# Key halves and head scaling moved between engines, scores kept negated, eps as a 129th square: a hybrid decoder layer on one core

## The chip, the core and the metric

The kernel runs on one core of one Trainium2 chip, in fp32. The metric is the device time of one execution in microseconds (us). TensorE multiplies matrices into PSUM, VectorE and ScalarE work element by element on SBUF and PSUM, GpSimd on SBUF alone, and SyncE issues most DMA transfers. In the profile these are PE, DVE, ACT, POOL and SP. Each engine takes its instructions in order from a queue of its own.

## What is computed

One layer of a decoder, for a prompt of 1024 tokens behind 16 learned meta tokens, and for 8 decoding sequences of one token each with 4096 cached positions. The part that the change touches is the differential attention of the prompt: 4 heads, each with two softmax maps over keys of width 64, values of width 128, ALiBi slopes and a causal mask. The output of each head is normalised by its root mean square.

```python
def diff_attend(q, k, v, q_pos, k_pos, lam, slopes):
    s = jnp.einsum('bqhjd,bkhjd->bhjqk', q, k) * (HEAD_DIM ** -0.5)
    s = s - slopes[None, :, None, None, None] * dist
    s = jnp.where(k_pos[None, :] <= q_pos[:, None], s, NEG_INF)
    p = jax.nn.softmax(s, axis=-1)
    a = p[:, :, 0] - lam * p[:, :, 1]
    return jnp.einsum('bhqk,bkhe->bqhe', a, v)

def diff_head_out(o, lw, li):
    o = rms_norm(o, lw['subln']) * (1.0 - lambda_init_of(li))
    return o.reshape(o.shape[:2] + (ATTN_WIDTH,))
```

The projection before it, the convolution group beside it, the output projection and the SwiGLU feed-forward part behind it, and all of the decoding, are left as they are.

## The kernel before

The kernel is written out in full, without loops on the chip. A planner orders each engine's queue from the order in which the program names the work, its dependencies and its own estimate of durations; some work (convolution, cache pages) is named with a lower or higher priority. Three stages follow one another. First the input is normalised, transposed and split, and the projections for the convolution group run (to about 150 us). Then come the attention of the prompt, 4 heads of 8 blocks of 128 queries, with the rest of the convolution, the projections of the next heads and the first cache pages of the decoding beside it (about 150 to 510 us). Then the output projection, the feed-forward part and the rest of the decoding.

Full fp32 products are made of fp32r matmuls on split operands: a number is a rounded part H plus a remainder L. For the scores, the 128 rows of the contraction hold the 64 dimensions of a map twice. L1 holds H of the scaled query on one half of the partitions and L on the other. R1 holds the rounded key on both halves, R2 the key's remainder on both. Two matmuls, L1 with R1 and L1 with R2, give all four products (lines 502 and 503).

stripe_k makes the keys of a head in 3 chunks of columns. Of each chunk and map ScalarE makes the rounded key on its own half (line 296), VectorE the same on the other half (line 297), GpSimd the remainder on its own half (line 298), and VectorE the remainder on the other half (line 299). Lines 297 and 299 depend on the projected key and on line 296 only.

attn(h, i) does one block of queries. For each map TensorE makes the scores in pieces of at most 512 keys; VectorE adds the ALiBi term, scales by the slope and keeps a running maximum (line 504). Line 510 negates the two maxima, ScalarE takes the exponential with its sum (line 512), and VectorE combines the maps: a reciprocal (514), the factor for the second map (516), and the weighted sum over all keys (520). TensorE transposes the result (528), ScalarE copies it (532), and TensorE multiplies with the values (542). The blocks stay unnormalised: what is summed is the l0-fold of the output, where l0 is the first map's sum.

After every fourth block the 4 blocks are normalised: ScalarE copies them out of PSUM (550) and sums their squares (552), VectorE forms ssq/128 + eps*l0*l0 in two steps (556, 557), GpSimd takes the power -1/2 (559), and VectorE scales each block by it and by the weight row subln (561). Four blocks are one tile of 128x512, from a pool of 8 that other tiles use too. head_out transposes them (569), copies them out (571) and stores them; it is called in the next head's or half's work.

Beside this GpSimd multiplies cache pages with the decoding queries (line 677, two pages at a time), VectorE sums them (687), and the convolution's taps run on ScalarE (408), GpSimd (409) and VectorE (418). att_consts loads the weight row subln over all partitions and the page table early in the first stage (lines 366 to 369).

Of the kernel before, what the change touches and what calls it, by code (L numbers as in the profile page):

```python
# [16 lines left out]
P = 128  # L17
# [24 lines left out]
SLAB = 1056  # L42


@with_exitstack
def tile_layer(ctx: ExitStack, tc: tile.TileContext, I, O, cfg):
# [23 lines left out]
    def att(name, dt=F32):  # L70
        return at.tile([P, 512], dt, tag="at", name=name)
# [36 lines left out]
    subln = cst.tile([P, P], F32, name="subln")  # L108
    convb = cst.tile([P, 4], F32, name="convb")
# [174 lines left out]
    def stripe_k(h):  # L284
# [5 lines left out]
        for c, o in proj(HL, f"pk{h}"):  # L290
            key_evac(k, o, c, 4 + h, "s")
            c0, w = CHUNKS[c]
            d = slice(max(c0 - DB, 0), c0 + w - DB)
            for j in range(2):
                sl, ot = slice(j * HD, (j + 1) * HD), slice((1 - j) * HD, (2 - j) * HD)
                S.copy(R1s[j][sl, d], k[sl, d])
                V.tensor_copy(R1s[j][ot, d], k[sl, d])
                (G if cfg["r2_g"] else V).tensor_tensor(R2s[j][sl, d], k[sl, d], R1s[j][sl, d].bitcast(F32), op=ALU.subtract)
                V.tensor_tensor(R2s[j][ot, d], k[sl, d], R1s[j][sl, d].bitcast(F32), op=ALU.subtract)
            if c < 2:  # L300
                yield
# [64 lines left out]
    def att_consts():  # L366
        bcast_row(subln, I["subln_w"][0])
        V.tensor_scalar(subln, subln, 1.0 - LAM_INIT, None, op0=ALU.mult)
        D.dma_start(pts, I["page_table"].rearrange("(o b) n -> o (b n)", o=1))
# [111 lines left out]
    def attn(h, i):  # L481
        W = META + P * (i + 1)
        qs = slice(i * P, (i + 1) * P)
        if i == 0:
            att_st["l"] = smt(f"l{h}", 16, 2)
            att_st["ssq"] = smt(f"ssq{h}", 8, 2)
            if h == 0:
                att_st["junk"] = smt("junk", P, 1)
# [7 lines left out]
        mx = smt(f"mx{h}{i}", 2, 4)  # L496
        for j in range(2):
            p = slp.tile([P, NKEY], F32, tag="p", name=f"p{h}{i}{j}", bufs=cfg["p"])
            for a in range(0, W, w):
# [5 lines left out]
                    out=p[:, a:e], in0=o, in1=bias[:, b0 + a : b0 + e], scale=SLOPES[h],  # L505
                    scalar=NEG if a == 0 else mx[:, j : j + 1], op0=ALU.add, op1=ALU.max, accum_out=mx[:, j : j + 1],
                )
            pj.append(p)
        nm = smt(f"nm{h}{i}", 2, 4)
        V.tensor_scalar(nm, mx, -1.0, None, op0=ALU.mult)  # L510
        for j in range(2):
            S.activation(pj[j][:, :W], pj[j][:, :W], AF.Exp, bias=nm[:, j : j + 1], accum_out=lh[:, 2 * i + j : 2 * i + j + 1])
        rl = smt(f"rl{h}{i}", 1, 4)
        V.reciprocal(rl, lh[:, 2 * i + 1 : 2 * i + 2])
        cc = smt(f"cc{h}{i}", 1, 4)
        V.scalar_tensor_tensor(cc, lh[:, 2 * i : 2 * i + 1], neglam, rl, op0=ALU.mult, op1=ALU.mult)
# [30 lines left out]
        if i % 4 == 3:  # L547
            oh = att(f"oh{h}{i}")
            b0 = i - 3
            S.copy(oh, o)  # L550
            for b in range(4):
                S.activation(att_st["junk"], oh[:, b * P : (b + 1) * P], AF.Square, accum_out=ssq[:, b0 + b : b0 + b + 1])
            bs = slice(b0, i + 1)
            l0 = lh.rearrange("p (i j) -> p i j", j=2)[:, bs, 0]
            t1 = smt(f"t1{h}{i}", 4)
            V.scalar_tensor_tensor(t1, l0, EPS, l0, op0=ALU.mult, op1=ALU.mult)
            V.scalar_tensor_tensor(t1, ssq[:, bs], 1.0 / P, t1, op0=ALU.mult, op1=ALU.add)
            r = smt(f"or{h}{i}", 4)
            G.tensor_tensor(r, t1, mhalf[:, :4], op=ALU.pow)
            for b in range(4):  # L560
                V.scalar_tensor_tensor(
                    oh[:, b * P : (b + 1) * P], oh[:, b * P : (b + 1) * P], r[:, b : b + 1], subln,
                    op0=ALU.mult, op1=ALU.mult,
                )

            def head_out():
                pt = pb(f"oT{h}{i}")
                for b in range(4):
                    T.transpose(out=pt[:, b * P : (b + 1) * P], in_=oh[:, b * P : (b + 1) * P], identity=ident)
                m = att(f"mo{h}{i}")  # L570
                S.copy(m, pt)
# [860 lines left out]
```

## Time and profile before

| | |
|---|---|
| median of 3 runs | 1490.66 us (1486.98 to 1492.48) |
| the profiled execution | 1491.31 us |
| its span, from the first to the last instruction | 1489.3 us |
| busy: TensorE, VectorE, ScalarE, GpSimd | 1375.3, 964.9, 514.8, 562.6 us |
| mean granted TensorE clock | 0.960 |

The busy times are those of the span. The profile names instructions by line of the kernel and by tile (out<-in), and says for idle time which engine's instruction ended it. A line's duration includes what an instruction waits after its start. The granted clock is the share of full speed that TensorE had. The chain of waits is followed back from the last instruction: at each step to what released it, or to the instruction before it on its engine.

### The profile page before, as it was taken

Reading aid. Unit: us, or ns where it says so; the run is one execution under the profiler, and the core shown is the slowest. Engines: PE = TensorE matmul, PEld = TensorE weight load, DVE = VectorE, ACT = ScalarE, POOL = GpSimd, SP = SyncE. Lnnn points to the kernel's source line nnn. Section 1 sums busy time; section 2 is a strip of 40 time slices with the busy share of each in tenths; the row PEclk is TensorE's granted clock in tenths of the full one; section 3 lists DMA queues with packets and bytes.
Section 4 is the critical chain, followed back from the end, with each engine's and each line's share of the span. In section 5 each row is a group of like instructions: output and inputs, shape, how many; then the busy total and the mean of one; then the engine's idle time right before and its main releaser. Section 6 shows DMA issues by size and latency. Waiting matters only on the chain.

```text
span 1489.3 us, 21639 instructions
## 1 busy us (share of the span) xinstructions
PE 1375.3 (92%) x6960; PEld 1071.5 (72%) x6960; DVE 964.9 (65%) x1531; ACT 514.8 (35%) x1021; POOL 562.6 (38%) x351
## 2 busy tenths in 40 slices
PE   6999678888875899999999999999999999999997
PEld 6999678877864778777776776767676666566666
DVE  5689998894888456855665747575654176353158
ACT  6566565547555324511312012211112112112122
POOL 3698663542425211363554445455540000000014
PEclk9999899998886899999999999999999999999999
DMA  8211012422424554768886777677676735763454
GB/s 263 72 44 45 15 44 93 121 85 92 156 81 148 181 173 136 268 214 255 278 267 208 250 244 246 235 258 267 216 253 225 260 122 192 261 192 124 162 182 173
DMA packets 199534, 264.35 MB, mean 178 GB/s; under 512 B 16279, under 2 KB 99672, under 8 KB 199413
## 3 DMA queue, kind: packets, MB, share of 16 engines
q1 hardware_dynamic: 188768, 254.40, 52.2%
q10 hardware_dynamic: 10653, 8.57, 1.8%
q8 instruction: 55, 0.90, 0.2%
q14 instruction: 58, 0.48, 0.1%
HBM read 245.92 MB, written 17.48 MB: 177 GB/s over the span
## 4 chain that ended last, share of the span: by engine, by line
PE 68%; DVE 16%; issue 5%; DMA 4%; ACT 3%; SPq 2%; POOL 1%; DVEq 0%; POOLq 0%; ACTq 0%
PE pg L147 6%; PE pg L148 6%; PE pg L149 6%; PE pu L147 5%; PE pu L148 5%; PE pu L149 5%; PE dn L147 5%; PE dn L148 5%; PE dn L149 5%; PE pv L729 4%; DVE p L504 2%; PE mo L149 2%; PE mo L147 2%; PE mo L148 2%; DVE acc L418 2%
## 5 line engine op out<-in xcount | busy, mean ns | idle before, releaser
L677 POOL TENSOR_TENSOR k<-k,qB 128x1024 f32<-128x1024 f32 x128 | 320.5, 2518 | 269.1 <-DMA k<-in_cache_k 227.6
L687 DVE TENSOR_REDUCE s<-k 128x16 f32<-128x1024 f32 x128 | 154.8, 1212 | 99.8 <-POOL k L677 95.0
L953 ACT CAST wH<-wr 128x1024 fp32r<-128x1024 f32 x66 | 69.0, 1048 | 251.9 <-DVE wL L955 148.9
L147 PE MATMUL dn<-wH,aH 128*128 128x512 f32 x352 | 141.6, 406 | 4.2 <-DVE y L996 2.6
L147 PE MATMUL pu<-hH,wH 128*128 128x512 f32 x352 | 141.0, 401 | 1.3 <-DVE y L996 1.3
L149 PE MATMUL pu<-hH,wL 128*128 128x512 f32 x352 | 139.7, 398 | 1.5 <-DVE sm2n_t L121 1.5
L148 PE MATMUL dn<-wL,aH 128*128 128x512 f32 x352 | 140.9, 400 | 0.0
L148 PE MATMUL pu<-hL,wH 128*128 128x512 f32 x352 | 140.1, 399 | 0.0
L147 PE MATMUL pg<-hH,wH 128*128 128x512 f32 x352 | 140.1, 398 | 0.0
L149 PE MATMUL dn<-wH,aL 128*128 128x512 f32 x352 | 140.0, 398 | 0.0
L148 PE MATMUL pg<-hL,wH 128*128 128x512 f32 x352 | 139.6, 396 | 0.0
L149 PE MATMUL pg<-hH,wL 128*128 128x512 f32 x352 | 139.5, 396 | 0.0
L955 DVE TENSOR_TENSOR wL<-wr,wH 128x1024 fp32r<-128x1024 f32 x66 | 104.4, 1582 | 43.8 <-ACT wH L953 23.6
L996 DVE TENSOR_TENSOR y<-dn,y 128x512 f32<-128x512 f32 x144 | 95.0, 682 | 33.7 <-PE dn L149 33.4
L409 POOL TENSOR_TENSOR cb<-cb 128x512 f32<-128x512 f32 x80 | 103.6, 1325 | 26.5 <-ACT cb L408 14.2
L418 DVE SCALAR_TENSOR_TENSOR acc<-u,cw,acc 128x512 f32<-128x512 f32 x144 | 99.5, 748 | 0.3
L1068 POOL TENSOR_TENSOR y<-y,wfpost 128x512 f32<-128x512 f32 x10 | 17.3, 1747 | 207.1 <-ACT ft L1066 207.0
L147 PEld LDWEIGHTS dn<-wH,aH 128*128 128x128 f32 x352 | 67.6, 192 | 30.7 <-issue 6.9
L147 PEld LDWEIGHTS pu<-hH,wH 128*128 128x128 f32 x352 | 66.6, 189 | 28.8 <-issue 12.0
L148 PEld LDWEIGHTS dn<-wL,aH 128*128 128x128 f32 x352 | 67.2, 191 | 24.4 <-issue 10.3
L147 PEld LDWEIGHTS pg<-hH,wH 128*128 128x128 f32 x352 | 66.2, 188 | 24.9 <-issue 9.0
L148 PEld LDWEIGHTS pu<-hL,wH 128*128 128x128 f32 x352 | 66.5, 189 | 24.2 <-issue 10.3
(582 smaller groups left out, 2986.5 us busy)
## 6 DMA issues: line engine op xcount, KB each, us to landing
k<-in_cache_k SPq DMA_DIRECT2D x256, 256.0 KB
v<-in_cache_v SPq DMA_DIRECT2D x256, 256.0 KB
wr<-in_w_gate SPq DMA_DIRECT2D x22, 512.0 KB
wr<-in_w_up SPq DMA_DIRECT2D x22, 512.0 KB
wr<-in_w_down SPq DMA_DIRECT2D x22, 512.0 KB
sd<-in_w_down SPq DMA_DIRECT2D x22, 512.0 KB
sw_gate<-in_w_gate SPq DMA_DIRECT2D x20, 512.0 KB
sw_up<-in_w_up SPq DMA_DIRECT2D x20, 512.0 KB
```

Source lines behind the costliest of these rows:

```text
L147: T.matmul(out, lhsT=wH, rhs=xH, start=first, stop=False)
L148: T.matmul(out, lhsT=wH, rhs=xL, start=False, stop=False)
L149: mark(T.matmul(out, lhsT=wL, rhs=xH, start=False, stop=last))
L409: G.tensor_tensor(accp, accp, t, op=ALU.add)
L418: V.scalar_tensor_tensor(dst, src, cw[:, ct, k : k + 1], acc, op0=ALU.mult, op1=ALU.add)
L504: V.tensor_tensor_reduce(out=p[:, a:e], in0=o, in1=bias[:, b0 + a : b0 + e], scale=SLOPES[h], scalar=NEG if a == 0 else mx[:, j : j + 1], ...
L677: x = G.tensor_tensor(kt, kt, qB.unsqueeze(1).to_broadcast([P, 2, 512]), op=ALU.mult)
L687: x = V.tensor_reduce(s.rearrange("p a c -> p (a c)"), kt.rearrange("p a (c d) -> p (a c) d", d=HD), axis=AX.X, op=ALU.add)
L729: x = T.matmul(pv[32 * g : 32 * g + 8, :], lhsT=a[:, q + i, :], rhs=vt[:, i, :], start=q + i < 4, stop=q + i >= NPG - 4, tile_position=(0, ...
L953: S.copy(H[:, :1024], raw[:, :1024])
L955: V.tensor_tensor(L[:, :1024], raw[:, :1024], H[:, :1024].bitcast(F32), op=ALU.subtract)
L996: V.tensor_tensor(y[b][:, ws], o, y[b][:, ws], op=ALU.add)
```

## The change

The second halves of the key operands: line 297's copy goes from VectorE to ScalarE, reading the key as before. Line 299's subtraction on VectorE becomes a copy by ScalarE of what GpSimd's subtraction (line 298) gave on the other half. GpSimd keeps that subtraction.

The scores are kept with the sign turned: the slope is negative, the running maximum becomes a running minimum of the negated scores, which is the bias that the exponential needs; the exponential takes a scale of -1. Line 510 goes. The factor of line 516 is formed with two per-partition scalars instead of a scalar and a second tensor.

The normalisation: a tile of 4 x 132 columns with 2 buffers of its own holds the 4 blocks. ScalarE writes sqrt(128*eps)*l0 behind each block's 128 columns, and the square sums 129 columns, so that the power takes the sum as it is; lines 556 and 557 go. The factor sqrt(128) moves into the weight. ScalarE scales each block by the power (instead of VectorE, line 561). The weight subln, now one value a partition (a new load of 128 values and one multiplication in att_consts), is applied in the copy behind the transposition (line 571). The row form of subln stays, for the decoding.

```diff
--- before.py
+++ after.py
@@ -40,6 +40,7 @@
 C0 = CHUNKS[0][1]
 KT = [(0, META)] + [(META + P * i, P) for i in range(NB)]
 SLAB = 1056
+OHW = P + 4
 
 
 @with_exitstack
@@ -106,6 +107,7 @@
         D.dma_start(dst, row.partition_broadcast(P))
 
     subln = cst.tile([P, P], F32, name="subln")
+    sublnT = cst.tile([P, 1], F32, name="sublnT")
     convb = cst.tile([P, 4], F32, name="convb")
     clnw = cst.tile([P, 4], F32, name="clnw")
     clnb = cst.tile([P, 4], F32, name="clnb")
@@ -294,9 +296,9 @@
             for j in range(2):
                 sl, ot = slice(j * HD, (j + 1) * HD), slice((1 - j) * HD, (2 - j) * HD)
                 S.copy(R1s[j][sl, d], k[sl, d])
-                V.tensor_copy(R1s[j][ot, d], k[sl, d])
-                (G if cfg["r2_g"] else V).tensor_tensor(R2s[j][sl, d], k[sl, d], R1s[j][sl, d].bitcast(F32), op=ALU.subtract)
-                V.tensor_tensor(R2s[j][ot, d], k[sl, d], R1s[j][sl, d].bitcast(F32), op=ALU.subtract)
+                S.copy(R1s[j][ot, d], k[sl, d])
+                G.tensor_tensor(R2s[j][sl, d], k[sl, d], R1s[j][sl, d].bitcast(F32), op=ALU.subtract)
+                S.copy(R2s[j][ot, d], R2s[j][sl, d].bitcast(F32))
             if c < 2:
                 yield
         for pt, ts, name in key_tiles(k, f"kn{h}"):
@@ -366,6 +368,9 @@
     def att_consts():
         bcast_row(subln, I["subln_w"][0])
         V.tensor_scalar(subln, subln, 1.0 - LAM_INIT, None, op0=ALU.mult)
+        with nc.allow_non_contiguous_dma("128 values, once"):
+            D.dma_start(sublnT, I["subln_w"][0].rearrange("(p o) -> p o", o=1))
+        S.mul(sublnT, sublnT, (1.0 - LAM_INIT) * P ** 0.5)
         D.dma_start(pts, I["page_table"].rearrange("(o b) n -> o (b n)", o=1))
 
     def conv_consts():
@@ -485,7 +490,7 @@
             att_st["l"] = smt(f"l{h}", 16, 2)
             att_st["ssq"] = smt(f"ssq{h}", 8, 2)
             if h == 0:
-                att_st["junk"] = smt("junk", P, 1)
+                att_st["junk"] = smt("junk", P + 1, 1)
         lh, ssq = att_st["l"], att_st["ssq"]
         L1s, R1s, R2s = heads[h]["L1"], heads[h]["R1"], heads[h]["R2"]
         bias = att_st["alibi"]
@@ -493,7 +498,7 @@
         np_ = -(-W // 512)
         w = -(-W // np_ // 8) * 8
         pj = []
-        mx = smt(f"mx{h}{i}", 2, 4)
+        nm = smt(f"nm{h}{i}", 2, 4)
         for j in range(2):
             p = slp.tile([P, NKEY], F32, tag="p", name=f"p{h}{i}{j}", bufs=cfg["p"])
             for a in range(0, W, w):
@@ -502,18 +507,19 @@
                 T.matmul(o, lhsT=L1s[j][:, qs], rhs=R1s[j][:, a:e], start=True, stop=False)
                 T.matmul(o, lhsT=L1s[j][:, qs], rhs=R2s[j][:, a:e], start=False, stop=True)
                 V.tensor_tensor_reduce(
-                    out=p[:, a:e], in0=o, in1=bias[:, b0 + a : b0 + e], scale=SLOPES[h],
-                    scalar=NEG if a == 0 else mx[:, j : j + 1], op0=ALU.add, op1=ALU.max, accum_out=mx[:, j : j + 1],
+                    out=p[:, a:e], in0=o, in1=bias[:, b0 + a : b0 + e], scale=-SLOPES[h],
+                    scalar=-NEG if a == 0 else nm[:, j : j + 1], op0=ALU.add, op1=ALU.min, accum_out=nm[:, j : j + 1],
                 )
             pj.append(p)
-        nm = smt(f"nm{h}{i}", 2, 4)
-        V.tensor_scalar(nm, mx, -1.0, None, op0=ALU.mult)
         for j in range(2):
-            S.activation(pj[j][:, :W], pj[j][:, :W], AF.Exp, bias=nm[:, j : j + 1], accum_out=lh[:, 2 * i + j : 2 * i + j + 1])
+            S.activation(
+                pj[j][:, :W], pj[j][:, :W], AF.Exp, scale=-1.0, bias=nm[:, j : j + 1],
+                accum_out=lh[:, 2 * i + j : 2 * i + j + 1],
+            )
+        cc = smt(f"cc{h}{i}", 1, 4)
         rl = smt(f"rl{h}{i}", 1, 4)
         V.reciprocal(rl, lh[:, 2 * i + 1 : 2 * i + 2])
-        cc = smt(f"cc{h}{i}", 1, 4)
-        V.scalar_tensor_tensor(cc, lh[:, 2 * i : 2 * i + 1], neglam, rl, op0=ALU.mult, op1=ALU.mult)
+        V.tensor_scalar(cc, lh[:, 2 * i : 2 * i + 1], neglam, rl, op0=ALU.mult, op1=ALU.mult)
         A = pj[0]
         cut = META + 3 * P
         for a, e in (((0, cut), (cut, W)) if W > cut and cfg["asp"] else ((0, W),)):
@@ -545,30 +551,26 @@
                 )
         mark(x)
         if i % 4 == 3:
-            oh = att(f"oh{h}{i}")
+            oh = at.tile([P, 4 * OHW], F32, tag="oh", name=f"oh{h}{i}", bufs=2)
+            ov = oh.rearrange("p (b e) -> p b e", e=OHW)
             b0 = i - 3
-            S.copy(oh, o)
-            for b in range(4):
-                S.activation(att_st["junk"], oh[:, b * P : (b + 1) * P], AF.Square, accum_out=ssq[:, b0 + b : b0 + b + 1])
+            S.copy(ov[:, :, :P], o.rearrange("p (b e) -> p b e", e=P))
             bs = slice(b0, i + 1)
             l0 = lh.rearrange("p (i j) -> p i j", j=2)[:, bs, 0]
-            t1 = smt(f"t1{h}{i}", 4)
-            V.scalar_tensor_tensor(t1, l0, EPS, l0, op0=ALU.mult, op1=ALU.mult)
-            V.scalar_tensor_tensor(t1, ssq[:, bs], 1.0 / P, t1, op0=ALU.mult, op1=ALU.add)
+            S.mul(ov[:, :, P], l0, (P * EPS) ** 0.5)
+            for b in range(4):
+                S.activation(att_st["junk"], ov[:, b, : P + 1], AF.Square, accum_out=ssq[:, b0 + b : b0 + b + 1])
             r = smt(f"or{h}{i}", 4)
-            G.tensor_tensor(r, t1, mhalf[:, :4], op=ALU.pow)
+            G.tensor_tensor(r, ssq[:, bs], mhalf[:, :4], op=ALU.pow)
             for b in range(4):
-                V.scalar_tensor_tensor(
-                    oh[:, b * P : (b + 1) * P], oh[:, b * P : (b + 1) * P], r[:, b : b + 1], subln,
-                    op0=ALU.mult, op1=ALU.mult,
-                )
+                S.mul(ov[:, b, :P], ov[:, b, :P], r[:, b : b + 1])
 
             def head_out():
                 pt = pb(f"oT{h}{i}")
                 for b in range(4):
-                    T.transpose(out=pt[:, b * P : (b + 1) * P], in_=oh[:, b * P : (b + 1) * P], identity=ident)
+                    T.transpose(out=pt[:, b * P : (b + 1) * P], in_=ov[:, b, :P], identity=ident)
                 m = att(f"mo{h}{i}")
-                S.copy(m, pt)
+                S.mul(m, pt, sublnT)
                 if h < NH - 1:
                     S.dma_start(mixT[h, :, b0 * P : (i + 1) * P], m)
                 else:
```

## Rows read from the trace of the kernel before

**Rows 1.** Stretch: us, busy PE, PEld, DVE, ACT, POOL (count), clock, DMA share, GB/s.

```profile
0.00:150.00 150.00, 135.85 (x851) 132.24 (x851) 113.82 (x202) 94.54 (x157) 105.07 (x99) 0.98 0.35 105
150.00:510.00 360.00, 282.32 (x1684) 260.77 (x1685) 296.90 (x630) 201.14 (x506) 160.12 (x105) 0.87 0.31 98
510.00:1489.30 979.30, 957.12 (x4427) 678.47 (x4425) 554.20 (x700) 219.09 (x359) 297.44 (x148) 0.99 0.66 218
```

**Rows 2.** The same view, first and last part of the attention stage.

```profile
150.00:220.00 70.00, 51.09 (x283) 46.69 (x283) 69.29 (x130) 41.31 (x96) 45.08 (x34) 0.88 0.11 31
...
450.00:500.00 50.00, 30.58 (x154) 26.17 (x155) 38.15 (x72) 22.64 (x53) 26.49 (x13) 0.66 0.39 133
```

**Rows 3.** Chain of waits, shares by line, in 150:220 and in 220:510.

```profile
by line: DVE acc L418 38.1%; issue 12.2%; DVE p L504 11.1%; DVE R L297 9.0%; DVE R L299 7.6%; DVE nm L510 6.6%; DVE p L520 6.0%; DVE acc L416 2.9%; DVE L L268 2.1%; DVE acc L410 2.0%; DVE u L418 1.2%; DVE cc L516 0.9%; DVE rl L514 0.6%; DVE
...
by line: issue 11.7%; DVE p L504 8.1%; DVE p L520 6.6%; PE o L542 5.1%; ACT p L512 4.9%; DVE R L299 4.8%; DVE cc L516 4.2%; DVE R L297 3.6%; DVE oh L561 3.2%; DVE s L687 2.9%; PE AT L528 2.5%; PE S L502 1.9%; DMA k<-in_cache_k 1.8%; ACT u L
```

**Rows 4.** Who waited for whom, 150:510: us in total, times, longest.

```profile
ACT p L512 <- DVE nm L510: 43.4, 20, 9.4
...
PE S L502 <- DVE mx L504: 20.7, 13, 4.6
...
POOL k L677 <- DMA k<-in_cache_k: 21.1, 1, 21.1
...
DVE t L557 <- ACT junk L552: 12.9, 4, 5.8
...
ACT cb L408 <- POOL cb L409: 3.5, 6, 0.9
```

**Rows 5.** VectorE groups, 150:510: count | busy us, mean ns | idle before, releaser.

```profile
L520 DVE SCALAR_TENSOR_TENSOR p<-p,cc,p 128x400 f32<-128x400 f32 (+7 forms) x52 | 40.8, 816 | 0.5
...
L299 DVE TENSOR_TENSOR R<-kT,R 64x384 fp32r<-64x384 f32 (+1 forms) x24 | 22.7, 946 | 0.7
...
L516 DVE SCALAR_TENSOR_TENSOR cc<-l,neglam,rl 128x1 f32<-128x1 f32 x32 | 20.2, 631 | 0.3
...
L297 DVE CAST R<-kT 64x384 fp32r<-64x384 f32 (+1 forms) x24 | 19.5, 817 | 0.6
...
L561 DVE SCALAR_TENSOR_TENSOR oh<-oh,or,subln 128x128 f32<-128x128 f32 x32 | 16.7, 583 | 2.4 <-POOL or L559 2.3
...
L510 DVE TENSOR_SCALAR nm<-mx 128x2 f32<-128x2 f32 x32 | 16.7, 525 | 0.3
...
L557 DVE SCALAR_TENSOR_TENSOR t<-ssq,t 128x4 f32<-128x4 f32 x8 | 5.4, 674 | 12.9 <-ACT junk L552 12.9
...
L556 DVE SCALAR_TENSOR_TENSOR t<-l 128x4 f32<-128x4 f32 x8 | 4.5, 558 | 2.6 <-ACT p L512 2.6
```

**Rows 6.** Single lines: count, shortest/median/longest ns, first and last start, forms.

```profile
L297 DVE CAST R<-kT x24: 296/791/2521, 150.9 to 412.3; 64x384 fp32r<-64x384 f32 x16, 64x272 fp32r<-64x272 f32 x8
...
L510 DVE TENSOR_SCALAR nm<-mx x32: 149/170/2379, 166.9 to 476.7; 128x2 f32<-128x2 f32 x32
...
L561 DVE SCALAR_TENSOR_TENSOR oh<-oh,or,subln x32: 339/347/2431, 220.9 to 505.6; 128x128 f32<-128x128 f32 x32
...
L121 DVE TENSOR_SCALAR hr_t<-hs x8: 135/154/155, 515.9 to 603.2; 128x1 f32<-128x1 f32 x8
```

**Rows 7.** ScalarE groups as in rows 5; the last as in rows 6.

```profile
L296 ACT CAST R<-kT 64x384 fp32r<-64x384 f32 (+1 forms) x24 | 11.3, 480 | 0.5
...
L552 ACT ACTIVATE junk<-oh 128x128 f32<-128x128 f32 x32 | 9.9, 308 | 1.5 <-ACT junk L552 1.0
...
L436 ACT ACTIVATE u<-yT,ln0n,ln_r x4: 450/457/460, 240.1 to 241.1; 128x128 f32<-128x128 f32 x4
```

**Rows 8.** GpSimd groups, 150:510, as in rows 5.

```profile
L677 POOL TENSOR_TENSOR k<-k,qB 128x1024 f32<-128x1024 f32 x25 | 59.5, 2389 | 28.3 <-DMA k<-in_cache_k 21.1 <-issue 7.0
...
L298 POOL TENSOR_TENSOR R<-kT,R 64x384 fp32r<-64x384 f32 (+1 forms) x24 | 23.5, 984 | 43.5 <-ACT R L296 35.4 <-PE S L502 7.4
```

**Rows 9.** ScalarE timeline around 56 us: start, us, instruction, idle before and releaser.

```profile
55.91 1.05 ACT L136 CAST wi8H<-wi8r 128x1024 fp32r<-128x1024 f32 x1 [2.96 <-DMA wi8r<-in_w_in]
```

## Prediction

> **What bounds the kernel now.** I read the busy times by stretch first. After 510 us TensorE is busy 957 of 979 us at a granted clock of 0.99; up to 150 us it is busy 136 of 150. Between them, 150 to 510 us, where the four heads' attention runs beside the convolution and the first cache pages, it is busy 282 of 360 at 0.87, while VectorE has 297 (82%), ScalarE 201 (56%) and GpSimd 160 (44%) [rows 1]. Everything the change touches but one load runs in that stretch, so only this stage is to be judged. At its start it is plain who sets the pace: in 150 to 220 us VectorE is busy 69.3 of 70 us. [...]
>
> The chain of waits says the same. In the first 70 us it goes through VectorE nearly throughout, from 220 on mostly through VectorE, with pieces of TensorE and ScalarE between [rows 3]. And the waits show the direction: TensorE waits for the scores' reduction to free PSUM (20.7 us for its scores alone), ScalarE waits 43.4 us in 20 places for the negated maximum; ScalarE waits for GpSimd hardly at all (3.5 us in 6 places, in the convolution's taps) [rows 4]. So VectorE is the engine to relieve here, and ScalarE has about 159 us free.
>
> **What VectorE loses.** Within 150 to 510 us: L297 19.5 us, L299 22.7, L510 16.7, L561 16.7, L556 4.5 and L557 5.4 go; together 85.5 us. L516 stays as an instruction without a second tensor; a 128x1 tensor_scalar took at most 155 ns [rows 6], so its 20.2 us may become 32 x 0.155 = 5.0, a gain of 15.2 (bounds 0 and 15.2) [rows 5]. Sum 100.7 us of 297.
>
> But most of that is waiting inside the instruction. L510, two elements wide, takes 149 ns at best and 2379 at worst; L297 296 to 2521; L561 339 to 2431 [rows 6]. The long ones have the length of GpSimd's page product, 2389 ns [rows 8]. By the shortest durations the removed work is 48 key copies and subtractions x 0.296 = 14.2, 32 x 0.149 = 4.8 for L510, 16 x 0.149 = 2.4 for L556 and L557, 32 x 0.339 = 10.8 for L561, together 32 us; L516 would gain about nothing. So 32 us is work, and 100.7 - 32 = 69 us is waiting for GpSimd, a wait that can pass on to the next instruction of the same kind. L520 is that next one: it stands right behind L516, has two SBUF inputs, and has 52 instructions of mean 816 ns [rows 5]. I take it that a third of the waits move there: 212 instructions (those of rows 5) shrink to 52, but the 52 meet the same GpSimd work.
>
> [...]
>
> **What ScalarE gains.** A 64-partition cast of the same shape takes it 480 ns [rows 7]. The first copy: 24 x 0.48 = 11.5. The second, from the subtraction's result: 24 x 0.48 = 11.5. The heads' scaling, 32 pieces of 128x128 with a per-partition scale: between the square with no such operand, 308 ns, and the normalisation with two, 457 ns; I take the middle, 0.38, so 12.2 (9.9 to 14.6). The scaled row sum, 8 pieces, at most as long as the square: 2.5. The copy after the transposition gets a per-partition scale: 8 x 0 to 0.15, 0.6. Sum 38 us, into 159 free.
>
> **Costs near nothing.** The exponential takes an immediate scale of -1 and a minimum takes the place of a maximum: same instruction, same count. Eps goes into a 129th column of the square, 1 element more. GpSimd keeps its 24 subtractions (984 ns) and 8 powers; each power is now released by ScalarE's sum and no longer by L557, which waited 12.9 us for that sum [rows 4]. One new load, 128 values on SyncE's queue among the loads of the first 60 us, and one ScalarE multiplication that waits for it: the nearest row is ScalarE's wait of 2.96 us for a weight block at 56 us [rows 9]; 0 to 3 us, and TensorE, 136 of 150 us busy there with projections, has work queued, so I take 0. If that cover is gone it costs those 3 us.
>
> **The new waits.** L299 needed only ScalarE's first copy. Now ScalarE's second copy waits for GpSimd's subtraction, and the scaling waits for GpSimd's power; behind either, in ScalarE's queue, stand the exponentials and the copies of transposed weights, for which TensorE waits. There are 24 + 8 such handovers. From below: ScalarE lost 3.5 us in 6 places over the taps, where its multiplications alternate with GpSimd's sums [rows 4], and VectorE 2.3 us before L561 [rows 5]; the planner that orders each queue puts other work between. From above: each of 12 chunks (4 heads, 3 chunks) holds ScalarE for two subtractions, 12 x 1.97 = 24 us. I take 5, well inside the 43 us that ScalarE idled for L510.
>
> **The sum.** What the chain loses: in 150 to 220 us L297 9.0%, L299 7.6%, L510 6.6% and L516 0.9%, 24.1% of 70 = 16.9 us; in 220 to 510, L299 4.8%, L516 4.2%, L297 3.6% and L561 3.2%, 15.8% of 290 = 45.8 us [rows 3]. Together 62.7; of L516's 12.8 a quarter remains as work, so 59.5. Of this, work and the two thirds of waits that vanish: (32 + 46) / 100.7 x 59.5 = 46 us. What comes back: 38 + 5 us on ScalarE, which ends at about (201 + 43) / 323 = 76% busy, below VectorE's old 82%; I put a quarter of the 38 on the path, 9 us, the handovers being inside it (bounds 0 and 43). 46 - 9 = 37 us. The profiled execution took 1491.3 us, 1489.3 of it span; its place against the median of the runs, 1490.7, is 0.6 above. 1491.3 - 37 = 1454 us. After 510 TensorE is full, so what the stage saves should stay saved to the end; the page loads are paced by TensorE's work and run at 0.66 share there [rows 1].
>
> **The rivals.**
> Waits move on: all 69 us of waiting reappear at L520 and its like. Then the chain loses 32 / 100.7 x 59.5 = 19 us, less 9 to 15 on ScalarE: 1482 to 1487, say 1485. For it: nothing about GpSimd's work changes. Against it: three quarters of the instructions that can meet it go.
>
> ScalarE takes VectorE's place: the 43 us lie on its path nearly in full, 46 - 37 = 9 us left: 1482. For it: the subtraction's handover is in the loop of each key chunk, and head 0's are needed at once. Against it: 159 us free.
>
> Slower: ScalarE stops behind a page. GpSimd's queue holds 25 page products; one waited 21.1 us for its page [rows 4, 8]. If a subtraction or power of the above stands behind such a product, ScalarE stands still too, and with it exponentials and transposes. Each costs about 21.1 + 2.4 = 23.5 us. One leaves the forecast at 1478; from two on the gain of 37 is eaten: 2 x 23.5 - 37 = +10, 1501. For it: a shorter stage asks for pages earlier. Against it: once in 25 so far.
>
> More: nothing comes back, 60 us, 1431. TensorE would then run its 282 us, fewer at a better clock, in 300, which the stage after 510 shows to be possible.
>
> The change doesn't do what it says: if ScalarE's half copies or scaled pieces took twice the rows' durations, nothing would be left, 1491; a 64-partition row of the same shape makes that unlikely.
>
> **How the numbers follow.** Forecast 0.57 (about 1437 to 1473); waits move on 0.11; ScalarE in VectorE's place 0.10; more 0.11; slower 0.09; not as said 0.02. The range reaches from the end of "more" to that of "waits move on", 1428 to 1486, and leaves out the slower rival and the tails. A measurement of this kernel can tell about 0.5%, 7.5 us: faster means under 1483, slower over 1498. Faster: 0.57 + 0.11 + half of the two small-gain rivals, 0.11 = 0.79; within: 0.10 + 0.02 = 0.12; slower 0.09.
>
> **What would show it.** Right: in the attention stage VectorE's busy time falls by 70 to 90 us, ScalarE's rises by about 38, the wait of the exponentials falls far below 43 us, the stage ends 37 us earlier, at about 473, and the time after it stays 979 us. L516 stays near 0.15 us with no long cases. L520's mean shows how much waiting moved: 816 ns plus a third of 69 us over 52, some 1250; twice that would be the second rival. ScalarE's waits for GpSimd before the second copies and before the scaling show the handovers: 5 us expected, one stop over 15 us would be the slower rival at work. Wrong: the stage ends early but the part after it grows, or TensorE's idle time in the stage stays at 78 us under another name, say transposed weights' copies or a half clock through the end of the stage.

## The result and the profile after

The changed kernel took 1449.2 us (median of 4 executions, 1442.3 to 1453.7), the kernel before 1488.8 beside it: a ratio of 0.973, with an interval of 0.968 to 0.978. That is 39.6 us faster; the forecast was 1454, 37 us under the profiled execution of before. The profiled execution of the changed kernel is the fastest of its four, 1442.3 us, and that of before, 1491.3 us, lies 2.5 us above the median, so differences between the two traces come out some 9 us larger than those of the medians (49.0 against 39.6).

I take as the end of the attention stage the last transposition of normalised heads. Before, it started at 510.7 us and ended at 511.0; now it ends at 464.4. These are its rows before and after (shortest/median/longest ns, first and last start):

```profile
L569 PE MATMUL oT<-ident,oh x32: 270/418/475, 234.7 to 510.7; 128*128 128x128 f32 x32
...
L571 PE MATMUL oT<-ident,oh x32: 270/273/475, 216.7 to 464.1; 128*128 128x128 f32 x32
```

The busy times of the changed kernel in the attention stage and after it, columns as in rows 1:

```profile
150.00:464.40 314.40, 264.22 (x1700) 247.87 (x1699) 220.53 (x506) 239.71 (x599) 164.03 (x108) 0.93 0.36 114
464.40:1440.63 976.23, 954.05 (x4420) 675.41 (x4419) 544.46 (x700) 219.07 (x359) 292.79 (x147) 0.99 0.66 218
```

And the kernel before over its own stage, so that the same work is compared:

```profile
150.00:511.00 361.00, 283.32 (x1690) 261.63 (x1691) 297.30 (x631) 201.14 (x506) 160.98 (x106) 0.87 0.31 97
```

The stage lasts 314 us instead of 361, and the rest 976 instead of 978: in these two executions what the stage saved stayed saved. In the stage VectorE is busy 77 us less, ScalarE 39 us more, GpSimd 3 us more, and the granted clock is 0.93 instead of 0.87, so that TensorE does the same work in 264 us instead of 283. After the change TensorE is busy 84% of the stage, ScalarE 76%, VectorE 70%.

Groups of VectorE in the changed kernel's stage, which answer to rows 5 (line 526 was 520, line 522 was 516, line 432 belongs to the convolution's layer norm):

```profile
L526 DVE SCALAR_TENSOR_TENSOR p<-p,cc,p 128x400 f32<-128x400 f32 (+7 forms) x52 | 45.1, 898 | 0.7
...
L522 DVE TENSOR_SCALAR cc<-l,neglam,rl 128x1 f32<-128x1 f32 x32 | 8.5, 266 | 0.6
...
L702 DVE COPY s<-selfs 128x8 f32<-128x8 f32 x3 | 2.4, 870 | 0.0
...
L432 DVE SCALAR_TENSOR_TENSOR ln4n<-ln4m,ln_r 128x1 f32<-128x1 f32 x1 | 2.3, 2333 | 0.2 <-POOL ln_r L125 0.2
...
L432 DVE SCALAR_TENSOR_TENSOR ln3n<-ln3m,ln_r 128x1 f32<-128x1 f32 x1 | 2.3, 2331 | 0.2 <-POOL ln_r L125 0.2
...
L432 DVE SCALAR_TENSOR_TENSOR ln6n<-ln6m,ln_r 128x1 f32<-128x1 f32 x1 | 2.3, 2320 | 0.2 <-POOL ln_r L125 0.2
```

The weighted sum rose from 816 to 898 ns only. Line 522 has no long cases left, but costs 266 ns rather than 155. Some long cases turned up in places nobody named: three one-column instructions of the layer norm take 2.3 us now (before, one of them took 2.3 us, the same line for the decoding 2.2 and another 1.2), and copies of 8 columns 870 ns on average instead of 158.

Groups of ScalarE, answering to rows 7 (298, 299 and 301 are the key halves, 566 the scaling, 573 the copy with the weight; 150 to 470 us):

```profile
L301 ACT CAST R<-R 64x384 fp32r<-64x384 f32 (+1 forms) x24 | 11.5, 481 | 0.6
...
L299 ACT CAST R<-kT 64x384 fp32r<-64x384 f32 (+1 forms) x24 | 11.5, 481 | 0.6
...
L298 ACT CAST R<-kT 64x384 fp32r<-64x384 f32 (+1 forms) x24 | 11.5, 481 | 0.4
...
L566 ACT ACTIVATE oh<-oh,or 128x128 f32<-128x128 f32 x32 | 10.3, 393 | 6.1 <-POOL or L564 6.1
...
L573 ACT ACTIVATE mo<-oT,sublnT 128x512 f32<-128x512 f32 x8 | 5.5, 690 | 5.8 <-PE oT L571 5.8
```

And the waits that answer to rows 4:

```profile
ACT p L515 <- DVE nm L509: 19.4, 12, 5.3
...
DVE p L509 <- PE S L508: 33.2, 16, 8.5
...
PE S L507 <- DVE nm L509: 15.1, 7, 5.2
...
ACT oh L566 <- POOL or L564: 6.1, 3, 4.2
```

This is the kernel before for the second of them:

```profile
DVE p L504 <- PE S L503: 8.0, 7, 2.4
```

The exponentials wait 19 us for VectorE instead of 43. VectorE now waits 33 us for scores from TensorE instead of 8; TensorE still waits 15 us for VectorE's reduction, 21 before. ScalarE waits for GpSimd's power 6.1 us in 3 places, and before line 301, which waits for GpSimd's subtraction, 0.6 us in all.

### The profile page after: what moved, and what is told of

Its sections match the earlier page's. It is cut to its first block, busy times and chain, and to the rows that moved or that the text cites. A ratio compares the mean times of both kernels' runs of the same rounds, so it can differ in the third digit from the quotient of the medians.

```text
span 1440.6 us, 21580 instructions
## 1 busy us (share of the span) xinstructions
PE 1353.5 (94%) x6960; PEld 1054.5 (73%) x6960; DVE 876.8 (61%) x1403; ACT 552.2 (38%) x1112; POOL 560.5 (39%) x351
## 4 chain that ended last, share of the span: by engine, by line
PE 61%; DMA 2%; issue 2%; DVE 2%; SPq 2%; POOL 1%; ACT 0%; POOLq 0%; DVEq 0%; ACTq 0%
PE pg L149 5%; PE pu L149 5%; PE pg L150 5%; PE pu L150 5%; PE pu L151 5%; PE pg L151 5%; PE dn L149 5%; PE dn L150 5%; PE dn L151 5%; PE pv L731 4%; PE mo L151 2%; PE mo L149 2%; PE mo L150 2%; DMA k<-in_cache_k 1%; POOL k L679 1%
## 5 line engine op out<-in xcount | busy, mean ns | idle before, releaser
L957 DVE TENSOR_TENSOR wL<-wr,wH 128x1024 fp32r<-128x1024 f32 x66 | 97.1, 1471 | 38.0 <-ACT wH L955 21.6
L998 DVE TENSOR_TENSOR y<-dn,y 128x512 f32<-128x512 f32 x144 | 95.0, 684 | 35.4 <-PE dn L151 34.9
L981 ACT CAST aH<-sg 128x512 fp32r<-128x512 f32 x44 | 27.3, 621 | 163.2 <-DVE sg L974 163.1
L150 PEld LDWEIGHTS dn<-wL,aH 128*128 128x128 f32 x352 | 66.9, 190 | 25.1 <-issue 10.3
```

The lines of the kernel that those rows point to most:

```text
L150: T.matmul(out, lhsT=wH, rhs=xL, start=False, stop=False)
L957: V.tensor_tensor(L[:, :1024], raw[:, :1024], H[:, :1024].bitcast(F32), op=ALU.subtract)
L981: S.copy(aH, sg)
L998: V.tensor_tensor(y[b][:, ws], o, y[b][:, ws], op=ALU.add)
```

## Experiments

The theory to be tested: VectorE's queue sets the pace of the attention stage, so what leaves VectorE shortens it, until another engine takes over. Rivals: the waits for GpSimd only move to the next instruction; ScalarE takes VectorE's place; or the planner's new order moves the time by itself, whatever the edit. Times are medians; the difference is to the kernel before on the same chip, whose medians in the four sets of runs lie between 1488.8 and 1491.5 us. Stage ends and busy times are those of one execution of each kernel, the profiled one; the stage ends with the last transposition of heads.

### Each part alone

**Key halves alone** (b_keys): of the diff only

```diff
-                V.tensor_copy(R1s[j][ot, d], k[sl, d])
+                S.copy(R1s[j][ot, d], k[sl, d])
...
-                V.tensor_tensor(R2s[j][ot, d], k[sl, d], R1s[j][sl, d].bitcast(F32), op=ALU.subtract)
+                S.copy(R2s[j][ot, d], R2s[j][sl, d].bitcast(F32))
```

> The kernel before with the key halves' part alone (lines 297 and 299 by ScalarE). Theory of the prediction (VectorE's queue sets the pace of the attention stage, two thirds of the waits for GpSimd vanish): these lines held 36 us of the chain, so 36 x 0.77 = 28 us less, and 6 us back on ScalarE: 22 us faster than before. Waits move on to the weighted sum: only the work goes, about 6 us faster. Planner's order alone: anything within 10 us either way, unrelated to the part's size.

1450.6 us, 40.9 less (ratio 0.973, 0.971 to 0.975). This one part gives as much as the whole change, within the intervals. The stage ends at 472.1; its row:

```profile
150.00:472.10 322.10, 273.11 (x1700) 253.83 (x1699) 249.00 (x585) 230.19 (x563) 164.27 (x108) 0.90 0.34 111
```

VectorE is busy 48 us less in it, more than the 42 of the two lines. The gain is nearly twice the 22 us expected.

**Negated scores alone** (b_neg):

```diff
-                    scalar=NEG if a == 0 else mx[:, j : j + 1], op0=ALU.add, op1=ALU.max, ...
+                    scalar=-NEG if a == 0 else nm[:, j : j + 1], op0=ALU.add, op1=ALU.min, ...
...
-        V.tensor_scalar(nm, mx, -1.0, None, op0=ALU.mult)
```

with the negative slope and the exponential's scale of -1 as in the whole change.

> The kernel before with the negated scores alone (line 510 gone). Theory of the prediction: about 4 to 6 us faster, the exponentials' wait for VectorE falls from 43 us, and most of line 510's 16.7 us leaves VectorE. Waits move on: line 516 and the weighted sum take over what line 510 waited for GpSimd, under 2 us faster. Planner's order alone: within 10 us either way.

1473.1 us, 18.4 less (0.989, 0.987 to 0.991), three to four and a half times what was expected. The stage ends at 490.3:

```profile
150.00:490.30 340.30, 278.58 (x1690) 257.36 (x1691) 283.27 (x599) 201.15 (x506) 164.48 (x106) 0.89 0.32 104
```

VectorE lost 14 of line 510's 16.8 us; the stage became 21 us shorter. The wait of the exponentials, which was to fall, hardly changed (43.4 to 41.8 us). That speaks for VectorE's time as what counted, and not for the negation's place before the exponential:

```profile
ACT p L510 <- DVE nm L504: 41.8, 24, 5.3
```

**Line 516 alone** (b_cc):

```diff
-        V.scalar_tensor_tensor(cc, lh[:, 2 * i : 2 * i + 1], neglam, rl, op0=ALU.mult, op1=ALU.mult)
+        V.tensor_scalar(cc, lh[:, 2 * i : 2 * i + 1], neglam, rl, op0=ALU.mult, op1=ALU.mult)
```

> The kernel before with line 516 alone changed to two per-partition scalars. Theory of the prediction: its mean falls from 631 ns to about 155, some 7 us faster. Waits move on: its mean falls too, but the weighted sum's mean rises by as much in total, from 816 to about 1100 ns, and the time stays as it was. Planner's order alone: within 10 us either way.

1481.0 us, 10.5 less (0.993, 0.991 to 0.995). Its instructions (shortest/median/longest ns) and the weighted sum's group:

```profile
L516 DVE TENSOR_SCALAR cc<-l,neglam,rl x32: 257/271/274, 179.0 to 473.7; 128x1 f32<-128x1 f32 x32
...
L520 DVE SCALAR_TENSOR_TENSOR p<-p,cc,p 128x400 f32<-128x400 f32 (+7 forms) x52 | 42.4, 842 | 0.4
```

No case over 274 ns, where the old form had taken up to 2415; and the weighted sum right behind it went from 816 to 842 ns, 1.4 us in total. Here the wait did not move to the next instruction. The mean of line 516 was to fall to 155 ns and fell to 270. The stage ends at 501.2, VectorE is busy 289.3 us in it, 8.0 less than before.

**Normalisation alone** (b_heads):

```diff
-                V.scalar_tensor_tensor(
-                    oh[:, b * P : (b + 1) * P], oh[:, b * P : (b + 1) * P], r[:, b : b + 1], subln,
+                S.mul(ov[:, b, :P], ov[:, b, :P], r[:, b : b + 1])
...
-                S.copy(m, pt)
+                S.mul(m, pt, sublnT)
```

and lines 556 and 557 gone, with the 129th column and the new tile as in the whole change.

> The kernel before with the normalisation's part alone (eps in the square sum, scaling by ScalarE, the weight behind the transposition). Theory of the prediction: line 561 held 9.3 us of the chain, so 9.3 x 0.77 = 7 us less and 3 us back on ScalarE, 4 us faster, and lines 556 and 557 a little more. Waits move on: 3 us faster at most. ScalarE in VectorE's place: the wait of the scaling for GpSimd's power stops the exponentials, no gain or up to 5 us slower.

1485.3 us, 6.2 less (0.996, 0.994 to 0.997). The stage ends at 500.1, 11 us earlier, with VectorE busy 289.7 us; the rest took 984 instead of 978. Here most of what left VectorE came back: the lines taken out held 26.6 us (16.7, 5.4 and 4.5), VectorE is only 7.7 us lighter, and the weighted sum alone rose by 10.9 us, from 816 to 1023 ns:

```profile
L525 DVE SCALAR_TENSOR_TENSOR p<-p,cc,p 128x400 f32<-128x400 f32 (+7 forms) x52 | 51.7, 1023 | 0.7
```

The four add up to 76 us, the whole change gives 40. They are not independent.

### The planner's order, and a wait taken out by itself

**Another pool** (b_pool): nothing moves between engines.

```diff
-            oh = att(f"oh{h}{i}")
+            oh = at.tile([P, 512], F32, tag="oh", name=f"oh{h}{i}", bufs=2)
```

> The kernel before with nothing moved: only the tile of the four heads' blocks comes from two buffers of its own instead of the common eight. If the planner's order by itself moves the time by 5 to 10 us, as the differences between the parts might suggest, this shows it. Theory now (the gains come from VectorE's queue): within 4 us of before.

1489.0 us against 1489.8: 0.9999 (0.998 to 1.002). The queues are ordered anew, the stage ends at 508.4 instead of 511.0, VectorE is busy 299.8 us, and the time stays. That is one order among many, but it gives no support to the planner as the cause of 10 to 40 us. It also shows how much a new order alone shifts: 2.5 us of VectorE's busy time.

**Line 510 without its waits** (b_nm2):

```diff
-        V.tensor_scalar(nm, mx, -1.0, None, op0=ALU.mult)
+        for j in range(2):
+            V.tensor_scalar(nm[:, j : j + 1], mx[:, j : j + 1], -1.0, None, op0=ALU.mult)
```

> The kernel before with line 510's one instruction on two columns made two instructions on one column each: more work for VectorE (32 more instructions of about 0.15 us), but a one-column tensor_scalar took at most 155 ns before. If waiting for GpSimd in line 510 is what cost time: the long cases go, busy time of the line falls from 16.7 to about 10 us, and 4 to 12 us of the 18 that leaving the line out gained. If the line's work, its place in VectorE's queue, cost the time: 2 to 5 us slower than before. If waits move on: the long cases go to line 516 and the weighted sum, no change or slightly slower.

1491.2 us against 1489.8, 1.0014 (0.9995 to 1.003): no gain. Its 64 instructions, and its stage, which ends at 505.6:

```profile
L511 DVE TENSOR_SCALAR nm<-mx x64: 127/146/156, 159.5 to 473.8; 128x1 f32<-128x1 f32 x64
```

```profile
150.00:505.60 355.60, 283.36 (x1695) 262.66 (x1694) 295.44 (x664) 207.76 (x514) 166.16 (x108) 0.88 0.30 99
```

The long cases went entirely: none over 156 ns, where the two-column instruction had reached 2379 [rows 6]. By the prediction's count 12 us of waiting (16.8 less 32 x 0.149) were taken out and 4.6 us of work put in (64 x 0.146 against 32 x 0.149), which should leave VectorE 7.5 us lighter. It is 1.9 us lighter: some 5.6 us, nearly half of the waits, came back elsewhere, in the weighted sum among others (905 ns), though a new order alone moved VectorE's busy time by 2.5 us in b_pool. So the length of a line in the profile, waits included, is not what one gains by taking out its waits alone. The stage ended 5.4 us earlier all the same, and the rest took 982 instead of 978 us; of a difference of this size in the stage the time shows nothing.

### What sets the pace afterwards

**Whole change without the key halves** (a_keys_v), **without the normalisation** (a_heads_v), **without the negated scores** (a_nm): the diffs above, turned round.

> The changed kernel with lines 297 and 299 back on VectorE, the other three parts kept. The parts alone gave 41 (keys), 18 (negated scores), 10 (line 516) and 6 us (normalisation) against the kernel before, together 76, while all four gave 40 to 42. Theory now: VectorE sets the pace only until enough is off it, then TensorE and ScalarE do; the three other parts still find VectorE full, so they add up nearly, 27 to 35 us under before: about 1460. If instead each part's time is the planner's luck, the result is anywhere between 1445 and 1490.

1458.4 us, 33.1 less than before (0.977, 0.974 to 0.980). The stage ends at 470.2, with VectorE busy 34 us less than before:

```profile
150.00:470.20 320.20, 267.24 (x1690) 250.32 (x1691) 263.31 (x552) 214.92 (x549) 167.57 (x106) 0.91 0.35 114
470.20:1455.35 985.15, 956.49 (x4420) 678.15 (x4418) 541.23 (x700) 219.25 (x359) 295.06 (x147) 0.99 0.65 216
```

> The changed kernel with the normalisation as before (scaling by VectorE, lines 556 and 557 back), the other three parts kept. Theory now: VectorE has room, ScalarE gets 13 us back: the same as the changed kernel within 4 us, 1445 to 1453. If ScalarE sets the pace now: 6 to 10 us faster than the changed kernel. If VectorE still sets it: 6 us slower, as the part alone gained.

1455.0 us, 36.5 less (0.976, 0.973 to 0.978); the stage ends at 474.7, VectorE busy 252.4 us:

```profile
150.00:474.70 324.70, 267.57 (x1693) 248.46 (x1692) 252.44 (x552) 227.44 (x558) 164.33 (x107) 0.93 0.34 109
```

"The same within 4 us" was missed: it is 5.8 us slower than the changed kernel and its stage 10.3 us longer, nearly the 10.9 that the part alone had taken off the stage, as was expected if VectorE still set the pace.

> The changed kernel with line 510's negation and the maximum back, the other three parts kept. Theory now: VectorE has room, so most of the 18 us that this part gained alone is not lost again, but the negation lies in the path from scores to exponential: 2 to 8 us slower than the changed kernel. If VectorE still sets the pace: 15 to 18 us slower.

1456.1 us, 35.4 less (0.976, 0.973 to 0.979). In its stage and rest:

```profile
150.00:465.70 315.70, 266.04 (x1690) 248.22 (x1691) 225.45 (x535) 233.33 (x593) 162.56 (x106) 0.91 0.36 115
465.70:1453.93 988.24, 958.45 (x4420) 678.63 (x4419) 543.81 (x700) 218.97 (x359) 295.72 (x147) 0.99 0.65 215
```

The three lie within 10 us of the changed kernel, and their intervals overlap its own. Still, the changed kernel with more work for ScalarE (a_act2, the next experiment), measured beside them, took 1447.1 to 1451.8 us, and every execution of the three lies above that (1452.2 to 1460.4). So each of these parts is worth some 6 to 10 us in the whole, though the three together add nothing to the key halves alone that can be measured. The negation, worth 21 us of stage alone, costs 1 us of stage here (465.7 against 464.4). What a_nm and a_keys_v lose besides lies after the stage: 988 and 985 us instead of 976. TensorE waits there longer for the value pages; these are the rows of a_nm, a_keys_v and the changed kernel, and then of a_act2 and a_heads_v, between 511 and 1440 us:

```profile
PE pv L730 <- DMA v<-in_cache_v: 11.7, 4, 3.7
```

```profile
PE pv L731 <- DMA v<-in_cache_v: 10.4, 8, 3.7
```

```profile
PE pv L731 <- DMA v<-in_cache_v: 5.8, 3, 4.7
```

```profile
PE pv L732 <- DMA v<-in_cache_v: 9.9, 7, 3.9
```

```profile
PE pv L730 <- DMA v<-in_cache_v: 9.6, 6, 3.6
```

This wait is 5 to 6 us longer in a_nm and a_keys_v, but also 4 us longer in a_act2 and a_heads_v, whose rest took 979 us. So it does not tell these kernels apart, and why the rest is 9 to 12 us longer in the first two is not shown; executions of one kernel differ by as much (the changed kernel's by 11).

**More work for ScalarE** (a_act2): the changed kernel with

```diff
                 S.copy(R1s[j][ot, d], k[sl, d])
+                S.copy(R1s[j][ot, d], k[sl, d])
```

> The changed kernel with line 299's copy of the key's second half done twice by ScalarE: 24 more instructions of 0.48 us, 11.5 us of ScalarE. The prediction put a quarter of ScalarE's added work on the path: 3 us slower than the changed kernel. If ScalarE sets the pace in the stage now: 8 to 12 us slower. If TensorE does alone: no change.

1448.8 us, 42.7 less than before (0.972, 0.970 to 0.974): 9.5 us of ScalarE more, and no difference to the changed kernel, where a quarter on the path would have been 3 us.

```profile
150.00:466.20 316.20, 266.99 (x1690) 249.83 (x1691) 215.85 (x504) 249.18 (x621) 165.30 (x106) 0.91 0.36 113
```

ScalarE is at 79% of the stage, and adding to its load costs nothing that shows.

**One tap less for VectorE** (a_taps12): the changed kernel with

```diff
-    behind=-400, w0=7, w1=7, ..., taps=11, ...
+    behind=-400, w0=7, w1=7, ..., taps=12, ...
```

> The changed kernel with one more of the convolution's 31 taps on ScalarE and GpSimd and one less on VectorE: 8 instructions of 0.75 us off VectorE, 8 of 0.72 us more on ScalarE and 8 of 1.3 us more on GpSimd, up to about 215 us. VectorE is still busy 67.5 of 70 us between 150 and 220 us in the changed kernel. If it still sets the pace there: 2 to 5 us faster than the changed kernel. If TensorE, 61 of 70 there now, or the taps' sums on GpSimd do: no change or up to 5 us slower.

1447.4 us, 42.4 less (0.972, 0.969 to 0.976), the same as the changed kernel. Between 150 and 220 us VectorE is busy 62.4 us in it instead of 67.5 (first row; the second is the changed kernel's), and the stage ends at 465.0, not earlier:

```profile
150.00:220.00 70.00, 59.97 (x357) 56.49 (x357) 62.43 (x131) 56.60 (x130) 57.10 (x42) 0.93 0.16 50
```

```profile
150.00:220.00 70.00, 61.44 (x386) 58.45 (x385) 67.52 (x147) 58.98 (x137) 48.21 (x38) 0.95 0.16 50
```

So VectorE does not by itself set the pace even where it is nearly full. The edit also loads GpSimd with 9 us more in this stretch, so that a small gain eaten up there is not ruled out.

**Less work for TensorE** (a_one_mm): the changed kernel, which here leaves the keys' remainders out of the scores, with

```diff
-                T.matmul(o, lhsT=L1s[j][:, qs], rhs=R1s[j][:, a:e], start=True, stop=False)
-                T.matmul(o, lhsT=L1s[j][:, qs], rhs=R2s[j][:, a:e], start=False, stop=True)
+                T.matmul(o, lhsT=L1s[j][:, qs], rhs=R1s[j][:, a:e], start=True, stop=True)
```

> The changed kernel without the second of the two score matmuls (the keys' remainders are made but not used): 112 matmuls of about 0.34 us less for TensorE in the attention stage, some 35 us of 270; the scores lose their low part. If TensorE sets the pace there now: 20 to 35 us faster than the changed kernel. If VectorE, ScalarE and the path between them still do: under 8 us faster. Mixed: 10 to 20.

1429.5 us, 60.3 less than before (0.960, 0.955 to 0.965) and 20 less than the changed kernel.

```profile
150.00:449.70 299.70, 248.43 (x1584) 230.96 (x1583) 224.21 (x505) 233.59 (x597) 162.08 (x107) 0.91 0.38 122
```

112 matmuls less brought TensorE's busy time down by 16 us, at a clock of 0.91 instead of 0.93, and the stage by 15; the busy share stays at 83%. The 35 us of the expectation are the recorded durations of line 508 (36.8 us in sum), which overlap with their neighbours'. Of the five kernels with VectorE at 68 to 75% and ScalarE at 74 to 79% of the stage (the changed kernel, a_nm, a_act2, a_taps12 and this one) it is the only one whose stage ends clearly earlier. So the stage now follows what is taken off TensorE, nearly one for one in busy time; against the 35 us it is the mixed case, at its upper end. Two things qualify it: the edit also shortens the way from each score's start to VectorE by one matmul, and the runs do not separate the two; and in the changed kernel TensorE still idles 50 us of the stage.

### The stage against VectorE's busy time

| kernel | VectorE in the stage | less than before | stage shorter by | time less by |
|---|---|---|---|---|
| b_pool | 299.8 | -2.5 | 2.6 | 0.8 |
| b_nm2 | 295.4 | 1.9 | 5.4 | -1.4 |
| b_heads | 289.7 | 7.7 | 10.9 | 6.2 |
| b_cc | 289.3 | 8.0 | 9.8 | 10.5 |
| b_neg | 283.3 | 14.0 | 20.7 | 18.4 |
| a_keys_v | 263.3 | 34.0 | 40.8 | 33.1 |
| a_heads_v | 252.4 | 44.9 | 36.3 | 36.5 |
| b_keys | 249.0 | 48.3 | 38.9 | 40.9 |
| a_nm | 225.5 | 71.9 | 45.3 | 35.4 |
| changed kernel | 220.5 | 76.8 | 46.6 | 39.6 |
| a_taps12 | 217.4 | 79.9 | 46.0 | 42.4 |
| a_act2 | 215.9 | 81.5 | 44.8 | 42.7 |

All in us. Up to some 35 us the stage follows VectorE's busy time at 1.2 to 1.5 for one (b_neg 20.7 / 14.0, b_heads 10.9 / 7.7, b_cc 9.8 / 8.0, a_keys_v 40.8 / 34.0); b_pool and b_nm2 show some 3 to 5 us of stage that it does not account for. From there on the stage moves little: from the three kernels with 34 to 48 us off VectorE to the four with 72 to 82, 24 to 48 us more bring 4 to 10 us. That is why four parts worth 76 us give 40.

## Why the prediction was right, and where its working was not

The time, 1449.2 us, lies 5 us under the forecast of 1454 and well inside the range. The mechanism, VectorE as the bound of the stage, held; that the number came so close is partly luck. Step by step:

**What bounds the stage.** Right. Every kernel that took 7 us or more off VectorE was faster, the reordering alone was not, and the rest of the execution stayed at 976 to 988 us. The stage was to end at about 473 and ended at 464, and TensorE's idle time in it fell from 78 to 50 us. Nor did a half clock last through its end: the granted clock, 0.50 between 455 and 475 us before, was 0.50 between 420 and 430 us in the changed kernel and 1.00 from 450 us to the end of the stage.

**What VectorE loses.** "70 to 90 us" was 76.8. The removed lines held 85.5 us and line 516 lost 11.7 (20.2 less 8.5), together 97; by line, VectorE's other instructions rose by some 14 us. (The rest of the way from 97 to 77 is overlap: neighbouring records overlap by some 0.05 us, so that the lines add up to 328 us before, and the busy time is 297.) So about a fifth of the 69 us of waiting moved on, and not a third. The place was wrong too. The weighted sum was to rise to about 1250 ns (to twice that if all waits moved on, the "second rival") and rose to 898, 4.3 us in total; as much went into the small copies, some 3 us into the layer norm. Nor did waiting need two SBUF inputs, which the prediction gives for the weighted sum: lines 297 and 510, with one, took up to 2521 and 2379 ns. The split into work and waiting was off as well: it priced all 48 key instructions at 0.296 us, which is the shortest copy of 272 columns; of 384 columns a copy took 0.35 and a subtraction 0.55 at best (0.30 and 0.43 of 272), and by these figures the work was about 38 us instead of 32 and the waiting 63. Line 516 was sized from a row with constants, 155 ns; with two per-partition scalars it takes 266, so 8.5 us instead of 5.0.

**What ScalarE gains.** 38 us were expected, 38.6 measured (201.1 to 239.7). The scaling took 393 ns (0.38 expected), the copy with the weight 690 instead of 585. Of the quarter of it that was put on the path, 9 us, the runs show no sign: a_act2 put another 9.5 us on ScalarE for nothing, on top of the change.

**The handovers.** 5 us expected, 6.1 + 0.6 measured, the longest 4.2; the slower rival's stop of over 15 us did not come.

**The sum.** It was right in total by two errors against each other. The parts, taken by their shares of the chain, were too small: 22 us for the keys (measured alone 40.9), 4 to 6 for line 510 (18.4), 7 for line 516 (10.5), 4 for the normalisation (6.2). The whole busy time of the lines, waits included, would have priced three of the four better (42, 16.8 and 11.7 us), but not the normalisation (26.6). My reading, not shown, is that the chain passes through an engine only where the last wait ended, while an engine at 82% also holds back steps that the chain shows under other names. And the sum had no ceiling: it added chain shares as if VectorE stayed the bound to the end. The ceiling is there, at 45 to 47 us of stage, where TensorE is at 84%; the prediction saw TensorE only in its rival "more", at 60 us. Had the parts been sized rightly without the ceiling, the forecast would have been 1415 us (1491.3 less 76), 13 us below its range.

**The rivals.** "Waits move on" holds in part, and most plainly in b_heads, where 26.6 us of lines went and VectorE got 7.7 us lighter, and in b_nm2, where nearly half of the waits came back and no time was gained. That the long cases are waits for GpSimd the trace of before shows: all seven cases of line 510 over 1 us end 0.02 to 0.03 us after a GpSimd instruction does, as here, at 362.90 and 362.87 us:

```profile
360.50 2.37 POOL L677 TENSOR_TENSOR k<-k,qB 128x1024 f32<-128x1024 f32 x1 [21.10 <-DMA k<-in_cache_k]
...
361.14 1.76 DVE L510 TENSOR_SCALAR nm<-mx 128x2 f32<-128x2 f32 x1
```

The waiting ends with the GpSimd instruction, and the longest cases have its length, 2.3 to 2.4 us on both sides; what makes an instruction wait so, the runs do not show. As a forecast of the time of the whole change, 1485, the rival failed, since most of the waits of the lines that left did not reappear. "ScalarE in VectorE's place" is refuted by the gain itself and by a_act2. "Slower" did not occur.

**Left open.** Why nearly half of the waits came back in b_nm2, more in b_heads (26.6 us of lines removed, 7.7 gone), about a fifth in b_neg (16.8 removed, 14.0 gone) and none in b_keys (42 removed, 48 gone) is not settled; with 2.5 us of scatter from a new order alone (b_pool) the smaller of these shares are not well known. It may depend on which instruction the new order puts under a GpSimd product. Nor is it shown what sets TensorE's last 50 us of idle time in the stage. Nearly half of it, 24 us, lies between 390 and 450 us, where no engine is full:

```profile
390.00:450.00 60.00, 35.89 (x205) 31.16 (x204) 39.64 (x91) 33.31 (x92) 29.02 (x14) 0.75 0.41 137
```

There the steps from one engine to the next may set the pace, and not the load of any of them. Why the part after the stage took up to 12 us longer in some kernels is open too.

## What to carry to other kernels

Where one engine is busy over four fifths of a stage and the others well under, price an edit by the busy time that it takes off that engine, part by part, as a first estimate only, since waits inside the instructions can come back in others (here between none of the busy time taken out and over two thirds), and then look for the ceiling: the sum holds only until another bound takes over. Here a single one of four parts, moving the key halves to ScalarE, came within 8 us of the ceiling in the stage, and the other three, each a clear gain alone, added nothing to the time that can be measured behind it. Moving work that is dearer on the engine that gets it (a copy of 64x384 takes ScalarE 512 ns, VectorE 350 at best) pays when that engine has room, and adding to its load is the cheapest test of whether it has.

## What the runs showed of the hardware

A two-column fp32 tensor_scalar between SBUF tensors took up to 2379 ns, its long cases ending with a GpSimd instruction, while the same instruction on one column did not wait so: in b_nm2 64 instructions took between 127 and 156 ns in the same stage, and in the kernel before five one-column instructions of line 121 ran from start to end while GpSimd was at work, none of them longer than 155 ns. A product with one per-partition scalar and a second one-column tensor took up to 2415 ns; with two per-partition scalars instead none of 32 took over 276. On the other side VectorE's cost grew with the scalars' kind: 154 ns with constants (line 121), about 270 with two per-partition ones (266 in the changed kernel, 269 in b_cc). A per-partition scale cost ScalarE about 85 ns on a 128x128 tile (308 to 393, against the square without one) and 105 ns on the 128x512 copy (585 to 690).
